# Seven products for eight in 13 pairs of weight blocks of the two output projections of a two-layer attention trunk

## The chip, the cores and the metric

The kernel runs on one core of one Trainium2 chip. The metric is the device time of one execution in microseconds (us). Three runs of the kernel before gave 1759.19, 1760.52 and 1760.68 us. Five engines take part: TensorE (PE) multiplies matrices, VectorE (DVE) and ScalarE (ACT) work on elements, GpSimd (POOL) issues most of the small transfers, and SyncE (SP) issues the large ones.

## The reference

The input x has 256 rows of 2048 columns. Layer A projects it to queries, keys, values and gates of 4096 columns each and runs chunked attention in 32 heads of 128. Layer B takes queries and gates, and shared keys and values, from the rows that layer A leaves, and runs a causal attention with forget gates. Each layer ends in an output projection from 4096 to 2048 columns, which is added to x:

```python
x = x + (o * silu(g)) @ a_w_out      # layer A: o is (256, 4096), a_w_out is (4096, 2048)
...
x = x + (o * silu(g)) @ b_w_out      # layer B, the same shapes
...
out = rms_norm(x, final_norm)        # over the 2048 columns
```

Everything is float32.

## The kernel before, in words

**The three products.** PE multiplies float32 numbers of a reduced format (fp32r) here, so each factor is split in two: `hi` is the number rounded to that format, `lo` is what is left. A product is made of three matmuls, x_hi·w_hi, x_hi·w_lo and x_lo·w_hi (`mm3`, L182). Each matmul multiplies 128 rows of K by a 128x512 piece of weights.

**The stream of weights.** All weights are read once from HBM, in blocks of 512 KB: 128 partitions x 1024 numbers, that is two chunks of K (`KB` = 2, called j = 0 and 1) of 512 output columns. SP issues one transfer for a block into a `raw` tile (L203). There are three such tiles (`RAW`), taken in turn, so the transfer of a block waits until the block three before it has been split. ACT writes `hi` (L237) and DVE writes `lo` = raw - hi (L238), into one of four pairs of tiles (`SPLIT`), and waits until PE is done with the block that was in it. Since the rows are two halves of 128 (t = 0 and 1), a block makes 2 (j) x 2 (t) x 3 = 12 matmuls. The class `Feed` keeps three blocks split ahead of PE.

**The output projections.** `ao` (layer A) and `bo` (layer B) have four units each, ao0 to ao3 and bo0 to bo3: a unit is 512 output columns, 16 blocks (0 to 15), and two accumulators in PSUM, acc0 and acc1, for the two row halves. `project` goes through the blocks in an order that is written out by hand, `ao_order` and `bo_order`: unit after unit, with one exception: the last block of bo0 comes eight blocks into bo1. In bo3 the last eight blocks (`LATE`) multiply only t = 0 at first; their t = 1 matmuls come at the very end, so the row half t = 0 can be finished while PE still works. Five of these blocks (8 to 12) stay in tiles of their own (`KEPT`, called keep8 to keep12).

**The residual tile.** Four blocks before the end of a unit, `load_xin` has SP load the 512 KB of x that the unit is added to into `xin` (L617). All units share one buffer of this tile: the load for the next unit waits until everything has read it.

- In ao, DVE adds the accumulators (L626) and SP stores the sum to HBM as x1 (`x1d`, L627). Layer B needs x1 turned by 90 degrees. For units 0 to 2 that goes by a transposition on DVE (`xinY`), transfers from POOL and splits (L148, L149) some blocks later. For unit 3, PE transposes (L167), right at the first block of the next stage, which is called bqg0.
- In bo, DVE adds (L762), ACT sums the squares (`junk`, L763), and DVE multiplies with the final gain into `xg` (L765). After unit 3, `finish_tile` (L776 to L788) makes the row factor out of four sums (`fin`), scales `xg` and stores it, first for t = 0 and then for t = 1.

**Order.** The program is written as one sequence; a scheduler of the framework assigns each engine its instructions in an order of its own making. Each engine takes its instructions strictly in that order, and an instruction that waits holds up all behind it. This holds for SP and its transfers too.

Of the kernel before, what the change touches and what calls it, by code (L numbers as in the profile page):

```python
# [49 lines left out]
BIG = 8  # L50
TERMS = 8
HEAT = 9
WAIT = 8
# [10 lines left out]
def r32(ap):  # L64
    return ap.bitcast(F32)
# [8 lines left out]
def trunk(ctx, tc, x, x_t, gains, a_w_in, a_rel, a_w_out, kv_w, f_w, f_b, b_w_in, b_w_out, final_norm, out):  # L74
# [98 lines left out]

    def mm3(acc, lhs, k, ts, hi, lo, nk, begun):

        parts = [(lhs.h(k), hi), (lhs.h(k), lo), (lhs.l(k), hi)]
        steps = [(t, i) for t in ts for i in range(3)]
        if k < KB:
            steps = [(t, i) for i in (0, 2, 1) for t in ts]
        for t, i in steps:  # L180
            x, w = parts[i]
            pe.matmul(acc[t], x[:, t * P:(t + 1) * P], w,  # L182
                      start=t not in begun, stop=k == nk - 1 and i == 2)
            begun.add(t)

    class Feed:
# [19 lines left out]
        def begin(self, first=None):  # L206
            spec, b = next(self.todo, (None, 0))
            if spec:
                load, *splits = self.also.get((spec["name"], b), (None, None, None))
                if load:  # L210
                    load()
                self.loaded.append((spec, b, self.load(spec, b, first), splits))

        def prepare(self, ahead=True, parts=(slice(None),)):
            if not self.loaded:
                self.begin()
            if not self.loaded:
                return
            spec, b, raw, (before, behind) = self.loaded.pop(0)
            if before:  # L220
                before()
# [41 lines left out]
        def get(self):  # L263
            self.fill()
            return self.ready.pop(0)

    def spec(name, w, nk, late=0, kept=0, g0=None):


        return dict(name=name, w=w, nk=nk, late=late, kept=kept, g0=g0)  # L270
# [13 lines left out]
    ao = [spec(f"ao{u}", a_w_out[u], KI) for u in range(4)]  # L284
    for sp_ in ao:
        todo += whole(sp_)
    for g in range(NG):
# [3 lines left out]
    for sp_ in qkvg[2 * NG:]:  # L291
        todo += whole(sp_)
    ao_order = [i for sp_ in ao for i in whole(sp_)]
    bo_order = [i for sp_ in bo for i in whole(sp_)]
    bo_order.insert(KI // KB + WAIT, bo_order.pop(KI // KB - 1))
    todo += bo_order
    feed = Feed(todo)
    order = iter(qkvg)

    class Unit:  # L300
# [8 lines left out]
        def step(self, b):  # L309
            hi, lo = feed.get()  # L310
            hold = b >= self.nk // KB - self.late
            if hold:
                self.held.append((b, hi, lo))
            for j in range(KB):
                mm3(self.acc, self.lhs, b * KB + j, range(1 if hold else NT), cols(hi, j), cols(lo, j), self.nk,
                    self.begun)
            self.left -= 1
            if not self.left:
                for b, hi, lo in self.held:
                    for j in range(KB):  # L320
                        mm3(self.acc, self.lhs, b * KB + j, [1], cols(hi, j), cols(lo, j), self.nk, self.begun)

# [8 lines left out]

    def project(lhs, order, begun, closed, sides):


        units = {}
        for sp_, b in order:
            u = int(sp_["name"][-1])
            if u not in units:
                units[u] = Unit(lhs, sp_)
            units[u].step(b)  # L340
            begun(u, b)
# [6 lines left out]
            if not units[u].left:  # L348
                more = closed(u, units[u].acc)
                if more:  # L350
                    sides.append(more)
        for side, _ in sides:
# [40 lines left out]

    def attention(g, biases, qk, vg, half, ocat, queues=(pool,) * NQ, line=(None, None), home=None):

# [60 lines left out]
        act.activation(hi, oT, AF.Copy)  # L456
        dve.tensor_sub(lo, oT, r32(hi))
        yield

# [79 lines left out]
    def side_a(g, accs):  # L539
# [16 lines left out]

        yield from attention(g, biases, qk, vg, halfA, oA, (pool, pool, pool, act), (2, 2), home)

# [59 lines left out]

    def ao_begun(u, b):
        if b == 11:  # L620
            load_xin(xf, u)

    def ao_closed(u, acc):
        cs, xin = slice(u * UN, (u + 1) * UN), xins.pop(u)
        for t in range(NT):
            dve.tensor_add(xin[:, t], acc[t], xin[:, t])  # L626
# [11 lines left out]

    project(oA, ao_order, ao_begun, ao_closed, [(prev, [2, 6, 2, 1])])
    tot1 = const.tile([P, NT], F32, name="tot1")  # L640
# [74 lines left out]
    def side_b(g, accs):  # L715
# [17 lines left out]
        evac_scaled(kv, 0, GC, rsB, qk[:, :, GC:])  # L733
        rest_of = attention(g, biases, qk, lambda: (v, gs), halfB, oB, line=(1, 2), home=home)
        next(rest_of)
# [66 lines left out]

    project(oB, bo_order, bo_begun, bo_closed, [(old, [1, 1, 0]), (prev, [4, 2, 1, 1, 1, 7, 2, 1])])

# [44 lines left out]
```

## Time and profile before

| what | value |
|---|---|
| runs before | 1759.19, 1760.52, 1760.68 us, median 1760.52 |
| profiled execution, its own time | 1762.27 us |
| its span | 1760.4 us |
| mean granted PE clock | 0.998 |
| PE busy in the span | 1746.0 us, 99% |
| DVE, ACT, POOL busy | 66%, 62%, 29% |
| HBM read | 351.05 MB, 202 GB/s over the span |

The busy time of an engine is the time in which an instruction of it was executing. Rows of a timeline give start, duration, engine, line, operation, what is written and read, and the shape. A row of a group gives line, engine, operation, shape and count, then total busy time and the mean of one in ns, then the idle time of the engine ahead of these instructions and what ended it. A name of a tile in a row leaves its numbers out, so `ao_raw` stands for all blocks of ao.

### The profile page before, as it was taken

What the parts mean: (1) busy time and instruction counts of PE and PEld (TensorE: products, weight loads), DVE (VectorE), ACT (ScalarE), POOL (GpSimd) and SP (SyncE); (2) the same over time, 40 slices, a digit from 0 to 9 for tenths busy, and PEclk for the clock granted to TensorE, in tenths of its full rate; (3) what the DMA queues carried; (4) which work ended last, traced back from release to release, by engine and by line L of the source; (5) the groups of instructions that cost most, each with busy time, mean ns of one, the idle gap of its engine ahead of it and who ended that gap; (6) DMA issues with size and microseconds to landing.
All of it is one profiled execution on the core that took longest, in us unless ns stands there. A gap on an engine that the chain in (4) does not pass through costs nothing.

```text
span 1760.4 us, 25526 instructions
## 1 busy us (share of the span) xinstructions
PE 1746.0 (99%) x8387; PEld 1533.1 (87%) x8387; DVE 1159.1 (66%) x1662; ACT 1084.1 (62%) x2063; POOL 515.7 (29%) x1071
## 2 busy tenths in 40 slices
PE   9999999999999999999999999999999999999997
PEld 7888888888888888888888888888888888888886
DVE  6666666666666666655666777777777777776654
ACT  6555555555555555555556777777777777765443
POOL 1333333333333333111104333333333333333000
PEclk9999999999999999999999999999999999999999
DMA  7867776777777777777766777777777777776665
GB/s 255 248 218 227 225 225 224 225 224 224 223 224 224 224 225 222 222 239 240 239 195 226 236 227 222 227 224 226 223 228 226 227 222 231 249 225 222 216 217 161
DMA packets 143652, 396.34 MB, mean 225 GB/s; under 512 B 31104, under 2 KB 38560, under 8 KB 143392
## 3 DMA queue, kind: packets, MB, share of 16 engines
q1 hardware_dynamic: 107472, 354.25, 63.8%
q0 software_dynamic: 32256, 37.29, 6.6%
q10 hardware_dynamic: 3792, 3.17, 0.6%
q8 instruction: 66, 1.08, 0.2%
q14 instruction: 66, 0.54, 0.1%
HBM read 351.05 MB, written 4.23 MB: 202 GB/s over the span
## 4 chain that ended last, share of the span: by engine, by line
PE 94%; DMA 2%; DVE 2%; ACT 1%; issue 0%; POOL 0%; SPq 0%; ACTq 0%; DVEq 0%; POOLq 0%
PE bkv_acc L182 19%; PE bqg_acc L182 19%; PE avg_acc L182 18%; PE aqk_acc L182 17%; PE ao_acc L182 9%; PE bo_acc L182 8%; DMA bo_raw<-in_b_w_out 1%; PE op L448 1%; PE s0p L414 1%; PE op L391 0%; PE s1p L390 0%; PE s1p L391 0%; PE op L392 0%; PE op L390 0%; PE s1p L392 0%
## 5 line engine op out<-in xcount | busy, mean ns | idle before, releaser
L363 POOL DMA_DIRECT2D sgZ<-sgY x512 | 250.9, 497 | 194.6 <-DVE sgY L360 96.5
L363 POOL DMA_DIRECT2D turned<-turned x448 | 219.9, 498 | 267.7 <-PE avg_acc L182 93.0
L233 DVE SCALAR_TENSOR_TENSOR bqg_lo<-bqg_raw,gain,bqg_hi 128x512 fp32r<-128x512 f32 x256 | 182.0, 747 | 97.1 <-ACT bqg_hi L232 97.0
L232 ACT ACTIVATE bqg_hi<-bqg_raw,gain 128x512 fp32r<-128x512 f32 x256 | 170.9, 714 | 114.1 <-PE bqg_acc L182 50.2
L238 DVE TENSOR_TENSOR avg_lo<-avg_raw,avg_hi 128x1024 fp32r<-128x1024 f32 x127 | 153.4, 1219 | 115.6 <-ACT avg_hi L237 115.5
L238 DVE TENSOR_TENSOR aqk_lo<-aqk_raw,aqk_hi 128x1024 fp32r<-128x1024 f32 x125 | 152.4, 1219 | 92.7 <-ACT aqk_hi L237 92.6
L233 DVE SCALAR_TENSOR_TENSOR bkv_lo<-bkv_raw,gain,bkv_hi 128x512 fp32r<-128x512 f32 x256 | 181.3, 748 | 45.3 <-ACT bkv_hi L232 42.3
L237 ACT ACTIVATE avg_hi<-avg_raw 128x1024 fp32r<-128x1024 f32 x127 | 132.5, 1055 | 124.5 <-PE aqk_acc L182 60.1
L182 PE MATMUL bqg_acc<-bqg_hi,x1Th 128*128 128x512 f32 x512 | 191.6, 384 | 0.0
L182 PE MATMUL aqk_acc<-aqk_hi,xTh 128*128 128x512 f32 x512 | 190.9, 383 | 0.2
L182 PE MATMUL aqk_acc<-aqk_lo,xTh 128*128 128x512 f32 x512 | 189.0, 379 | 1.2 <-DVE aqk_lo L238 1.2
L182 PE MATMUL avg_acc<-avg_hi,xTh 128*128 128x512 f32 x512 | 190.2, 382 | 0.0
L182 PE MATMUL avg_acc<-avg_lo,xTh 128*128 128x512 f32 x512 | 188.9, 379 | 0.3 <-DVE avg_lo L238 0.3
L182 PE MATMUL bqg_acc<-bqg_hi,x1Tl 128*128 128x512 f32 x512 | 189.1, 379 | 0.0
L182 PE MATMUL bkv_acc<-bkv_hi,x1Th 128*128 128x512 f32 x512 | 189.0, 379 | 0.0
L182 PE MATMUL aqk_acc<-aqk_hi,xTl 128*128 128x512 f32 x512 | 188.9, 379 | 0.0
L182 PE MATMUL avg_acc<-avg_hi,xTl 128*128 128x512 f32 x512 | 188.8, 379 | 0.0
L182 PE MATMUL bkv_acc<-bkv_lo,x1Th 128*128 128x512 f32 x512 | 188.8, 379 | 0.0
L182 PE MATMUL bkv_acc<-bkv_hi,x1Tl 128*128 128x512 f32 x512 | 188.8, 379 | 0.0
L182 PE MATMUL bqg_acc<-bqg_lo,x1Th 128*128 128x512 f32 x512 | 188.8, 379 | 0.0
L237 ACT ACTIVATE aqk_hi<-aqk_raw 128x1024 fp32r<-128x1024 f32 x125 | 131.5, 1052 | 91.9 <-PE avg_acc L182 44.0
L232 ACT ACTIVATE bkv_hi<-bkv_raw,gain 128x512 fp32r<-128x512 f32 x256 | 168.8, 711 | 27.9 <-PE bqg_acc L182 21.4
(205 smaller groups left out, 3442.4 us busy)
## 6 DMA issues: line engine op xcount, KB each, us to landing
bqg_raw<-in_b_w_in SPq DMA_DIRECT2D x128, 512.0 KB, 4.3
bkv_raw<-in_kv_w SPq DMA_DIRECT2D x128, 512.0 KB, 4.0
avg_raw<-in_a_w_in SPq DMA_DIRECT2D x127, 512.0 KB, 4.3
aqk_raw<-in_a_w_in SPq DMA_DIRECT2D x125, 512.0 KB, 3.4
ao_raw<-in_a_w_out SPq DMA_DIRECT2D x64, 512.0 KB, 4.2
bo_raw<-in_b_w_out SPq DMA_DIRECT2D x64, 512.0 KB, 4.2
sgZ<-sgY POOLq DMA_DIRECT2D x512, 40.0 KB, 4.0
turned<-turned POOLq DMA_DIRECT2D x448, 32.0 KB, 3.5
```

What stands on the lines that cost most here:

```text
L182: pe.matmul(acc[t], x[:, t * P:(t + 1) * P], w, start=t not in begun, stop=k == nk - 1 and i == 2)
L232: act.activation(hi[:, :, j], raw[:, :, j], AF.Copy, scale=gk)
L233: dve.scalar_tensor_tensor(lo[:, :, j], raw[:, :, j], gk, r32(hi[:, :, j]), op0=OP.mult, op1=OP.subtract)
L237: act.activation(hi[:, :, j], raw[:, :, j], AF.Copy)
L238: dve.tensor_sub(lo[:, :, j], raw[:, :, j], r32(hi[:, :, j]))
L363: queues[j].dma_start(out=r32(z)[j * SQ:(j + 1) * SQ, i], in_=y[i * SQ:(i + 1) * SQ, j])
L414: pe.matmul(s0p[:, i], q0[:, i], qkT[:, HG + i, 0], start=True, stop=True)
L448: pe.matmul(op[:, i, P:], v1[:, i * DH:(i + 1) * DH], pT[:, i, NT], start=False, stop=i == HG - 1)
```

## The change

Thirteen times, one block of a unit and the block with the same number of its neighbour are taken together as a *quad*. The two blocks hold four pieces of weights: B11 and B21 (unit a, j = 0 and 1), B12 and B22 (unit b). The rows hold four pieces of x: A11 and A12 (t = 0), A21 and A22 (t = 1). Plainly that is eight products, and 24 matmuls. The quad makes them out of seven products, so 21 matmuls, in the form of Strassen and Winograd: four sums of pieces of x, four differences of pieces of weights, and sums of products.

- **Loading and splitting.** `Quad.load` (L283) brings both blocks, two transfers of 512 KB, into one tile `quad0`, of which there is only one. `Quad.split` gives four items, 0 to 3: B11 with B21; the two differences in `quad1` (written at L289); B22; and two further differences, that are written over pieces of `quad0` (L290, L298). Item 2 is 128x512, the others are 128x1024. Each is split by ACT (L295, hi0 to hi3) and DVE (L296, lo0 to lo3) into the same four pairs of tiles as the blocks. Quads don't count towards the three raw tiles.
- **Products.** Three of the seven go straight to an accumulator of a unit. The other four, p1, p5, p6 and p7, are shared between accumulators, so they add up over all quads of a pair of units in four banks of PSUM that the attention uses, too. After the last quad of a pair, ACT copies p1, and four adds of DVE make the four corrections out of them (`comb`, L337 to L341), in the tile `quad1`. At the end of each unit DVE adds its half of them to `xin` (128x1024, L752 and L926) ahead of the accumulators (L754, L891).
- **Sums of x.** The four sums are made for the first five groups of heads in each attention (`sum_up`): five small operations on DVE and one on ACT more for each.
- **Order.** Quads take the place of blocks 0 to 2 of ao0 and ao1, of blocks 0 to 4 of ao2 and ao3, and of blocks 0 to 4 of bo2 and bo3; Q0 is the first quad of a pair. bo0 and bo1 have none. The order (a and b being the two units of a pair) is now, for ao0 and ao1: a3 to a14, b3, Q0, b4, b5, a15, Q1, b6 to b8, Q2, b9 to b15. For the other two pairs: a5 to a8, Q0, a9 to a11, Q1, a12 to a14, Q2, b5 to b7, Q3, a15, b8, b9, Q4, b10 to b15. Unit a now ends with the last quad.

Two places show what that does to the order on the engines. At the end of ao, SP stands as follows. Before, the residual tile of ao3 (here `xin_8058`) was loaded some nine transfers before the first block of bqg0, the first stage of layer B:

```order
L617 DMA xin_8058<-in_x 128x2x512
L203 DMA ao3_raw8_7862<-in_a_w_out 128x1024
...
L203 DMA ao3_raw15_7998<-in_a_w_out 128x1024
L203 DMA bqg0_raw0_8021<-in_b_w_in 128x1024
...
L203 DMA bqg0_raw5_8124<-in_b_w_in 128x1024
L627 DMA x1d_6770<-xin_8058 128x512 x2
```

Now the stores of ao2's sum (`xin_7841`) stand behind two blocks of bqg0, and the load for ao3 (`xin_8147`) another block later:

```order
L204 DMA ao3_raw15_8070<-in_a_w_out 128x1024
L204 DMA bqg0_raw0_8115<-in_b_w_in 128x1024
L204 DMA bqg0_raw1_8133<-in_b_w_in 128x1024
L755 DMA x1d_6808<-xin_7841 128x512 x2
L204 DMA bqg0_raw2_8153<-in_b_w_in 128x1024
L744 DMA xin_8147<-in_x 128x2x512
L204 DMA bqg0_raw3_8173<-in_b_w_in 128x1024
```

So this load moved from ahead of ao3's last eight blocks to behind them, and behind three blocks of bqg0. On PE, the transpositions of ao3's sum stood behind the first matmul of bqg0:

```order
L182 MATMUL ao_acc_7821<-ao_hi_8060,oAl_182 128x512
L182 MATMUL bqg_acc_8190<-bqg_hi_8078,x1Th_6772 128x512
L167 MATMUL xT_8142<-ident,xin 128x128
L167 MATMUL xT_8147<-ident,xin 128x128
L182 MATMUL bqg_acc_8191<-bqg_hi_8078,x1Th_6772 128x512
```

They now stand behind nine of them:

```order
L183 MATMUL ao_acc_7624<-ao_hi_8149,oAl_182 128x512
L183 MATMUL bqg_acc_8300<-bqg_hi_8167,x1Th_6810 128x512
...
L183 MATMUL bqg_acc_8300<-bqg_hi_8167,x1Tl_6812 128x512
L168 MATMUL xT_8232<-ident,xin 128x128
L168 MATMUL xT_8237<-ident,xin 128x128
L183 MATMUL bqg_acc_8301<-bqg_hi_8167,x1Tl_6812 128x512
```

The transpositions thus stand eight matmuls further on. The second place is the end of bo. Before, SP loaded the residual tile of bo3 (`xin_16633`) ten blocks from the end:

```order
L203 DMA bo3_raw5_16424<-in_b_w_out 128x1024
L617 DMA xin_16633<-x1d_6770 128x2x512
L203 DMA bo3_raw6_16454<-in_b_w_out 128x1024
...
L203 DMA bo3_raw15_16605<-in_b_w_out 128x1024
L788 DMA out_0<-xg0_15431 128x512 x2
```

Now it comes last, and Q4's two transfers (`bo_quad0`) stand behind the block for keep10:

```order
L204 DMA bo3_raw10_16681<-in_b_w_out 128x1024
L283 DMA bo_quad0_15582<-in_b_w_out 128x2x512 x2
L204 DMA bo3_raw11_16692<-in_b_w_out 128x1024
...
L204 DMA bo3_raw15_16779<-in_b_w_out 128x1024
L744 DMA xin_16823<-x1d_6808 128x2x512
L917 DMA out<-xg_15579 128x512 x2
```

On DVE, before, the splits of keep8 to block 15 ran one after the other, with nothing between them:

```order
L238 TENSOR_TENSOR bo3_keep11_16591<-bo3_raw11_16543,bo3_keep11_16591 128x1024
L238 TENSOR_TENSOR bo3_keep12_16602<-bo3_raw12_16560,bo3_keep12_16602 128x1024
L238 TENSOR_TENSOR bo3_lo13_16614<-bo3_raw13_16577,bo3_hi13_16613 128x1024
L238 TENSOR_TENSOR bo3_lo14_16624<-bo3_raw14_16594,bo3_hi14_16623 128x1024
L238 TENSOR_TENSOR bo3_lo15_16636<-bo3_raw15_16605,bo3_hi15_16635 128x1024
```

The same engine has this from Q4's first item on:

```order
L296 TENSOR_TENSOR quad_lo0_16711<-bo_quad0_15582,quad_hi0_16710 128x1024
L289 TENSOR_TENSOR bo_quad1_15583<-bo_quad0_15582 128x1024
...
L246 TENSOR_TENSOR bo3_keep11_16768<-bo3_raw11_16692,bo3_keep11_16768 128x1024
...
L296 TENSOR_TENSOR quad_lo3_16748<-bo_quad0_15582,quad_hi3_16747 128x1024
L246 TENSOR_TENSOR bo3_lo13_16804<-bo3_raw13_16760,bo3_hi13_16803 128x1024
L338 TENSOR_TENSOR bo_quad1_15583<-bo_quad1_15583,p6_16374 128x512
L246 TENSOR_TENSOR bo3_lo14_16814<-bo3_raw14_16771,bo3_hi14_16813 128x1024
L246 TENSOR_TENSOR bo3_keep12_16776<-bo3_raw12_16700,bo3_keep12_16776 128x1024
...
L926 TENSOR_TENSOR xin_16567<-xin_16567,bo_quad1_15583 128x1024
L246 TENSOR_TENSOR bo3_lo15_16826<-bo3_raw15_16779,bo3_hi15_16825 128x1024
```

The splits of the last blocks now share DVE with those of Q4, and with the corrections and the residual of bo2 (`xin_16567`). The diff, cut to its core (the code of `sum_up`, of `open` and of the names that only passed a parameter is left out):

```diff
     def mm3(acc, lhs, k, ts, hi, lo, last, begun):
...
         def begin(self, first=None):
             spec, b = next(self.todo, (None, 0))
-            if spec:
+            if isinstance(b, Quad):
+                b.load()
+                self.loaded += [(spec, (b, i), None, (None, None)) for i in range(4)]
+            elif spec:
...
         def refill(self):
-            while len(self.loaded) < RAW:
+            while sum(raw is not None for _, _, raw, _ in self.loaded) < RAW:
...
+    class Quad:
...
+        def load(self):
+            q = self.all
+            for r in range(2):
+                sp.dma_start(out=q.raw[:, :, r], in_=q.w[self.units[r]][self.b])
+
+        def split(self, i):
+
+            raw, t = self.all.raw, self.all.t
+            if not i:
+                dve.tensor_sub(t[:, 0], raw[:, :, 1], raw[:, :, :, 0])
+                dve.tensor_sub(raw[:, :, 1, 0], raw[:, :, 1, 1], t[:, 0, :, 0])
+            src = [raw[:, :, 0], t[:, 0], raw[:, :, 1, 1:], raw.rearrange("p a r j n -> p a (r j) n")[:, :, 1:3]][i]
...
+            act.activation(hi[:, :, :n], src, AF.Copy)
+            dve.tensor_sub(lo[:, :, :n], src, r32(hi[:, :, :n]))
+            if not i:
+                dve.tensor_sub(raw[:, :, 0, 1], raw[:, :, 0, 1], raw[:, :, 1, 0])
+            return hi, lo
...
+            if self.first:
+                q.p = [bank(n) for n in ("p1", "p5", "p7", "p6")]
...
+            w = feed.get()
+            prod(p1, x(0, 0), w, 0)
+            add(first, 0, x(1, 0), w, 1)
+            w = feed.get()
+            prod(p5, sx(0), w, 0)
+            prod(p7, sx(2), w, 1)
+            w = feed.get()
+            add(second, 0, sx(3), w, 0)
+            w = feed.get()
+            add(first, 1, x(1, 1), w, 0)
+            prod(p6, sx(1), w, 1)
+            if self.last:
...
+                act.activation(c[:, 0], p1, AF.Copy)
+                dve.tensor_add(c[:, 3], c[:, 0], p6)
+                dve.tensor_add(c[:, 2], c[:, 3], p5)
+                dve.tensor_add(c[:, 1], c[:, 3], p7)
+                dve.tensor_add(c[:, 3], c[:, 1], p5)
...
+            normal = a[:-1] + b[:3] + a[-1:] + b[3:]
...
+    ao_order = ao_quads.order(ao[0], ao[1], 3, 13) + ao_quads.order(ao[2], ao[3], QUADS, 4)
...
+    bo_order = whole(bo[0]) + whole(bo[1])
     bo_order.insert(KI // KB + WAIT, bo_order.pop(KI // KB - 1))
+    bo_order += bo_quads.order(bo[2], bo[3], QUADS, 4)
...
+        if g < QUADS:
+            quads.sum_up(oT)
...
-    def ao_begun(u, b):
-        if b == 11:
+    def ao_begun(u, left):
+        if left == 4:
             load_xin(xf, u)
...
+        dve.tensor_add(xin, xin, ao_quads.comb[:, u % 2 * NT:u % 2 * NT + NT])
...
-    def bo_begun(u, b):
-        if b == (11 if u else 14):
+    def bo_begun(u, left):
+        if left == (4 if u else 1):
             load_xin(x1d, u)
...
+        if u > 1:
+            dve.tensor_add(xin, xin, bo_quads.comb[:, u % 2 * NT:u % 2 * NT + NT])
```

More of the change, by code (lines that the diff above doesn't have):

```diff
@@ L51 @@
 TERMS = 8
+QUADS = 5
 HEAT = 9
@@ L182, in mm3 @@
             pe.matmul(acc[t], x[:, t * P:(t + 1) * P], w,
-                      start=t not in begun, stop=k == nk - 1 and i == 2)
+                      start=t not in begun, stop=last and i == 2)
             begun.add(t)
@@ L219, in prepare @@
             spec, b, raw, (before, behind) = self.loaded.pop(0)
+            if raw is None:
+                self.ready.append(b[0].split(b[1]))
+                self.refill()
+                return
             if before:
@@ new lines, in trunk, with __init__, order, open @@
+    class Quads:
+        def __init__(self, name, w):
+            self.name, self.w, self.sums = name, w, []
+        def order(self, first, second, n, lead):
+            a, b = ([(sp_, i) for i in range(n, sp_["nk"] // KB)] for sp_ in (first, second))
+            normal = a[:-1] + b[:3] + a[-1:] + b[3:]
+            units = [int(sp_["name"][-1]) for sp_ in (first, second)]
+            out = normal[:lead]
+            for i in range(n):
+                out.append((None, Quad(self, units, i, not i, i == n - 1)))
+                out += normal[lead + 3 * i:lead + 3 * i + 3] if i < n - 1 else normal[lead + 3 * i:]
+            return out
+        def open(self):
+            self.raw = big_tile([P, IL, 2, KB, HN], F32, f"{self.name}_quad0")
+            self.t = big_tile([P, 2, IL, KB, HN], F32, f"{self.name}_quad1")
+        def sum_up(self, oT):
+            if len(self.sums) % 2 == 0:
+                self.tile = big_tile([P, 2, 2, 4, P], F32R, f"{self.name}_sums{len(self.sums)}")
+            self.sums.append(self.tile[:, len(self.sums) % 2])
+            hi, lo = self.sums[-1][:, 0], self.sums[-1][:, 1]
+            v = att.tile([P, 4, P], F32, name="v_sums", tag="wideh")
+            a11, a21, a12, a22 = (oT[:, k, t * P:(t + 1) * P] for k in range(KB) for t in range(NT))
+            dve.tensor_add(v[:, 0], a21, a22)
+            dve.tensor_sub(v[:, 2], a11, a21)
+            dve.tensor_sub(v[:, 1], v[:, 0], a11)
+            dve.tensor_sub(v[:, 3], a12, v[:, 1])
+            act.activation(hi, v, AF.Copy)
+            dve.tensor_sub(lo, v, r32(hi))
@@ L313, in step @@
                 self.held.append((b, hi, lo))
+            self.left -= 1
             for j in range(KB):
-                mm3(self.acc, self.lhs, b * KB + j, range(1 if hold else NT), cols(hi, j), cols(lo, j), self.nk,
-                    self.begun)
-            self.left -= 1
+                mm3(self.acc, self.lhs, b * KB + j, range(1 if hold else NT), cols(hi, j), cols(lo, j),
+                    not self.left and j == KB - 1, self.begun)
             if not self.left:
@@ L330, in rest, with project, get @@
             yield u.acc
-    def project(lhs, order, begun, closed, sides):
+    def project(lhs, specs, order, begun, closed, sides):
         units = {}
+        def get(u):
+            if u not in units:
+                units[u] = Unit(lhs, specs[u])
+            return units[u]
         for sp_, b in order:
[L337 to L341, printed above, removed]
+            if sp_:
+                us = [int(sp_["name"][-1])]
+                get(us[0]).step(b)
+            else:
+                us = b.units
+                b.step(lhs, *(get(u) for u in us))
+            for u in us:
+                begun(u, units[u].left)
             for side, steps in sides:
@@ L347, in project @@
                         steps.pop(0)
[L348 to L351, printed above, removed]
+            for u in us:
+                if not units[u].left:
+                    more = closed(u, units[u].acc)
+                    if more:
+                        sides.append(more)
         for side, _ in sides:
```

43 lines of the change are left out of this document (32 added, 11 removed).

## The prediction

> **What bounds the kernel now.** I read the page first: its first part, and the shares of the chain that ended last.
>
> ```profile
> PE 1746.0 (99%) x8387; PEld 1533.1 (87%) x8387; DVE 1159.1 (66%) x1662; ACT 1084.1 (62%) x2063; POOL 515.7 (29%) x1071
> PE 94%; DMA 2%; DVE 2%; ACT 1%; issue 0%; POOL 0%; SPq 0%; ACTq 0%; DVEq 0%; POOLq 0%
> ```
>
> PE is busy for 99% of the span, and 94% of the last chain is PE. So I asked what PE waits for; the columns are total us, times, and the longest:
>
> ```profile
> PE op L390 <- ACT wideh L382: 1.9, 1, 1.9
> PE heat L108 <- DVE zeros L105: 1.3, 1, 1.3
> PE aqk_acc L182 <- DVE aqk_lo L238: 1.2, 2, 0.9
> PE bo_acc L182 <- DVE bo_lo L238: 0.8, 1, 0.8
> PE avg_acc L182 <- DVE avg_lo L238: 0.3, 1, 0.3
> ```
>
> That is 5.5 us in 1760. All splits and transfers are hidden behind matmuls. The time is the number of matmuls by their pace, plus the end. The pace is read from the timeline of ao, from the first to the last of 117 matmuls in a row:
>
> ```profile
> 839.76 0.38 PE L182 MATMUL ao_acc<-ao_hi,oAh 128*128 128x512 f32 x1
> ...
> 864.80 0.38 PE L182 MATMUL ao_acc<-ao_hi,oAl 128*128 128x512 f32 x1
> ```
>
> 25.04 us by 116 steps is 0.216 us (the 0.38 overlap). A block of 12 takes 2.59 us, a quad of 21 takes 4.53.
>
> **The change part by part.** *Matmuls removed.* 13 quads by 3 matmuls are 39, by 0.216: -8.4 us. This is all that the change can gain; each wait that it opens on PE is taken from that.
>
> *Work added to DVE and ACT.* The groups by shape give the means (ns, after the comma), and the DMA view of 770 to 860 us the transfers (us to landing, last); the row below those is a window at the start (us, then busy times; GB/s last).
>
> ```profile
> L238 DVE TENSOR_TENSOR ao_lo<-ao_raw,ao_hi 128x1024 fp32r<-128x1024 f32 x64 | 78.1, 1222 | 67.5 <-ACT ao_hi L237 67.2
> L457 DVE TENSOR_TENSOR oAl<-oT,oAh 128x512 fp32r<-128x512 f32 x16 | 11.1, 692 | 11.1 <-ACT oAh L456 11.1
> L626 DVE TENSOR_TENSOR xin<-ao_acc,xin 128x512 f32<-128x512 f32 x8 | 5.1, 682 | 0.0
> L765 DVE SCALAR_TENSOR_TENSOR xg<-xin,gfin 128x512 f32<-128x512 f32 x8 | 5.2, 684 | 0.1
> L149 DVE TENSOR_TENSOR x1Tl<-xinZ,x1Th 128x128 fp32r<-128x128 f32 x24 | 5.8, 284 | 0.0
> L237 ACT ACTIVATE ao_hi<-ao_raw 128x1024 fp32r<-128x1024 f32 x64 | 67.5, 1055 | 74.3 <-PE ao_acc L182 48.3 <-DMA ao_raw<-in_a_w_out 23.8 <-PE avg_acc L182 2.2
> L456 ACT ACTIVATE oAh<-oT 128x512 fp32r<-128x512 f32 x16 | 10.1, 630 | 31.3 <-DVE oT L452 31.3
> ...
> ao_raw<-in_a_w_out SPq DMA_DIRECT2D x35, 512.0 KB, 4.2
> x1d<-xin SPq DMA_DIRECT2D x4, 256.0 KB, 4.8
> xin<-in_x SPq DMA_DIRECT2D x2, 512.0 KB, 6.2
> ...
> 14.00:16.00 2.00, 2.00 (x11) 1.76 (x10) 1.77 (x4) 2.00 (x6) 0.00 (x0) 1.00 1.03 413
> ```
>
> No row shows the new subtractions; by shape they are nearest to the splits: 1.22 us for 128x1024, 0.69 for half of it. The sums of x in ten groups of heads cost DVE 4 x 0.28 + 0.69 and ACT 0.63 in each; DVE is busy for 66% and ACT for 62%, so I take 0 (0 to 0.5, for a group where a split comes late by it).
>
> A quad costs DVE four splits (3 x 1.22 + 0.69) and three differences (1.22 + 2 x 0.69), 6.95 us in all. With the three blocks between two quads that is 10.6 us, against 4.53 + 3 x 2.59 = 12.3 on PE. As throughput it fits. But there is one tile `quad0`: the next quad can be loaded only when lo3 has read it, and the loop through this tile is a first transfer, hi0 (1.06), and DVE's 6.95. (The second transfer lands 1.3 us after the first at the earliest, 512 KB at 413 GB/s, and hides behind hi0 and lo0.) With a transfer of 4.2 us, as for `ao_raw`, the loop is 12.2 us. That is 0.1 under PE's 12.3. Nine quads run in such a loop (two, four, and three of bo's; its Q4 is told below). Only where layer B's turned x comes in, 8 x 0.28 us of DVE work near the second pair's first quads, do I expect a wait: +0.7. The bounds are 0, and with 4.8 for a transfer (the x1d row) 9 x 0.5 = 4.5.
>
> *The end of ao.* T is when PE ends the last quad there. DVE must have split lo3 by then, and has three block splits queued behind; I take them as done at T+2. Then come three corrections (3 x 0.68), a block split (1.22), the fourth correction (0.68), the add to `xin` (1.22, as the split of that shape): T+7.2. Another block split and two accumulators: T+8.4, 9.1, 9.8. The stores of x1 land 4.8 us later, T+14.6. Only then can SP, where this load now stands behind ao3's last blocks, load `xin` for ao3, and three blocks of bqg0 wait behind it. At 4.2 us it lands at T+18.8; the two adds (1.22 + 0.68) bring it to T+20.7. PE reaches the transpositions after six blocks and nine matmuls, at T + 15.5 + 1.9 = 17.4. It waits for 3.3 us. Before, it lost some 0.3 here (a matmul of 0.22, then nothing until 879.10):
>
> ```profile
> 878.61 0.38 PE L182 MATMUL bqg_acc<-bqg_hi,x1Th 128*128 128x512 f32 x1
> ...
> 879.10 0.41 PE L167 MATMUL xT<-ident,xin 128*128 128x128 f32 x2
> ```
>
> So +3.0. The bounds: 1.2, if the stores land within the 3.0 us of the row for `out` below, and 5.0, if the load takes 6.2.
>
> *The end of bo.* These are the rows of its transfers, and of the end:
>
> ```profile
> out<-xg SPq DMA_DIRECT2D x4, 256.0 KB, 3.0
> xin<-x1d SPq DMA_DIRECT2D x1, 512.0 KB, 4.6
> ...
> 1740.13 0.48 PE L182 MATMUL bo_acc<-bo_lo,oBh 128*128 128x512 f32 x1 [0.78 <-DVE bo_lo L238]
> 1741.51 0.69 DVE L762 TENSOR_TENSOR xin<-bo_acc,xin 128x512 f32<-128x512 f32 x1 [1.44 <-PE bo_acc L182]
> 1745.05 0.16 DVE L781 SCALAR_TENSOR_TENSOR fin<-fin 128x1 f32<-128x1 f32 x1
> 1751.46 0.38 PE L182 MATMUL bo_acc<-bo_hi,oBl 128*128 128x512 f32 x1
> 1752.60 0.63 ACT L763 ACTIVATE junk<-xin 128x512 f32<-128x512 f32 x1 [6.02 <-DVE xin L762]
> 1753.13 0.19 ACT L763 ACTIVATION_READ_ACCUMULATOR junk<-xin 128x1 f32 x1
> 1754.13 0.16 DVE L781 SCALAR_TENSOR_TENSOR fin<-fin 128x1 f32<-128x1 f32 x1
> 1754.33 1.33 ACT L785 ACTIVATE xg<-xg,fin 128x512 f32<-128x512 f32 x2 [0.68 <-DVE fin L781]
> ```
>
> I count from U, when PE starts Q3. Without any new wait PE would take 2 x 4.53 for the quads, 2.59 for a15 and 8 x 2.59 for blocks 8 to 15, 32.4, then the wait of 0.8 that is there now, and 8.7 from the last matmul to the end of the span (1751.46 + 0.22 to 1760.4): U+41.9.
>
> Now the working of the new order. Between Q3 and Q4 stand a15 and only the t = 0 halves of blocks 8 and 9, so PE reaches Q4 at U + 4.5 + 2.6 + 2.6 = 9.7. By the loop above Q3's lo2 is done at U+1.0 (hi3 and lo3 of Q2 2.3 us after Q2's start, then 4.2 for the transfer, 1.06 for hi0 and 5.7 for DVE's six operations up to lo2, less 12.3); I take U+1.4, for the hand-overs. DVE then splits keep8 (U+2.6) and Q3's lo3 (U+3.9). Only now is the tile free. Q4's first transfer lands at U+8.1, hi0 at 9.2, lo0 at 10.4, the first differences at 12.3; DVE's order puts keep11's split there (13.5), then a difference (14.2), lo1, lo2 and lo3 (17.3). PE, with the last four matmuls behind lo3, ends Q4 at U+18.2, and with some hand-overs between ACT and DVE that I round up, at 18.5. Without the wait that would be U+15.1 (9.7 + 4.5, and four matmuls of keep8 that stand in between): 3.4 us.
>
> After it DVE has block 13 (18.6), a correction behind PE's last product (19.5), block 14, keep12 (21.9), three corrections (24.0), the add to bo2's `xin` (25.2), block 15 (26.5), two accumulators and two multiplications for `xg` (29.2, at 0.68 each). Then the tile is free, and the load for bo3 can start. It lands 4.2 us later (U+33.5; the `xin` row says 4.6, but nothing stands before it now). Add and accumulator: 35.4; from there to `fin` of t = 0 is 3.0 (1742.20 to 1745.21): 38.4. The accumulator of t = 1 follows in DVE's order (39.1), but ACT first scales `xg` (1.33: 39.7), then squares (0.8: 40.5); `fin` takes 1.0 (1753.32 to 1754.29), and from there to the end are 6.1 (1754.33 to 1760.4): U+47.6. That is +5.7 over 41.9; PE's wait of 3.4 is inside this. The bounds: 3.3, if Q4's transfer and the last load take 3.0 each, and 8, with 4.8 and a hand-over of 0.1 at each of ten steps.
>
> *Sum.* -8.4 + 0.7 + 3.0 + 5.7 = +1.0 us. The profiled execution has 1762.27 us of its own, and would have 1763.3. The median of the runs shown is 1.75 lower, 1760.52, and I add the same to that: **1761.5 us**. With the terms' bounds, seldom all on one side, this case runs from 1757 to 1767.
>
> **The rivals.** *Lone transfers land early* (faster). Both new waits are behind transfers that stand alone in SP's queue. The 4.2 us is measured with others under way, and 3.0 stands for stores of half the size, which speaks for some gain. Then the sum is -8.4 + 0 + 1.2 + 3.3 = -3.9, 1756.6; if PE waited nowhere, 1752.1. Against it: DVE's chain after Q4, 10 us of work in a written order, contains no transfer.
>
> *The tile of the quads becomes the bound* (slower). The place is `quad0`, the loop of 12.2 against 12.3 us. It decides from a first transfer of 4.3 us. Blocks now arrive five in 12.3 us, where there were 4.75, and the view gives 6.2 us for a load between others. At 5.2 us PE waits 0.9 in each of nine quads, 8.1 in place of 0.7: 1769. Against it: SP has waited for this tile, so few transfers are under way when it is loaded.
>
> *The clock falls in the new waits.* These are windows of the end; the column behind the engines is the granted clock.
>
> ```profile
> 1752.00:1753.00 1.00, 0.00 (x0) 0.00 (x0) 0.97 (x2) 0.40 (x1) 0.00 (x0) 1.00 0.00 0
> 1753.00:1754.00 1.00, 0.00 (x0) 0.00 (x0) 0.79 (x4) 0.62 (x3) 0.00 (x0) 1.00 0.00 0
> 1754.00:1755.00 1.00, 0.00 (x0) 0.00 (x0) 0.93 (x4) 0.67 (x2) 0.00 (x0) 0.59 0.00 0
> ```
>
> The clock falls about 2.3 us after the last matmul's end (1751.84). The longest wait in between, 1.9 us, left no trace. A wait of 3.3 us at the end of ao is longer than 2.3. If the clock then stays low for as long as PE stood, half of 3 us is lost, 1.5; twice, if Q4's pieces count as well: 1763 to 1764.5. Against it: at Q4 a few matmuls stand between the pieces of the wait. The Trainium skill (TensorE: Matmul & The Clock Gate, "HAM oscillation — how this bites in real kernels") says that PE must not idle for over some 3.4 us, or the clock is halved for the next window. By that rule a wait of 3.3 us is just short of costing anything, and one past it would cost 1.7 us, an estimate from that page. The trace agrees that idleness drops the clock; how long it stays low afterwards no row here shows.
>
> **How the numbers follow.** A measurement of this kernel can tell about 0.2%, 3.5 us, from no change: 1757 to 1764. Chances: the forecast 0.55, early transfers 0.2, the tile 0.15, the clock 0.1. Faster by over 0.2%: 0.04 of the forecast and 0.16 of early transfers, 0.20. Slower: 0.13 of the forecast (bounds of the two ends), 0.13 of the tile, 0.07 of the clock, 0.33. The rest, 0.47, is within it. The range is 1755 to 1768: it takes in the forecast's bounds, most of the early transfers and all of the clock, and leaves out the case of no waits and the worst of the tile, together under 0.2.
>
> **What would show it.** In the profile after, PE's matmuls should be 39 fewer; PE should wait for about 3 us at the transpositions behind bqg0's ninth matmul, released by DVE's add to `xin`, with SP's load waiting for x1d; for 3 us in pieces within bo's Q4; and the last matmul (U+18.5, 80 matmuls still to go, and a wait of about 1 for block 15, which makes U+36.8) should stand some 11 us ahead of the end of the span in place of 8.7. Waits of 0.5 us and more on lo0 or lo1 in each quad would mean the tile. A granted clock under 1.00 at 890 us would mean the clock. The forecast is wrong if the transpositions come without a wait, or if bo3's `xin` is loaded before the corrections of bo2 are done.

## The result and the profile after

| | before | after |
|---|---|---|
| median of 6 runs | 1760.60 us (1759.19 to 1763.19) | 1767.93 us (1766.77 to 1769.72) |
| profiled execution, its own time | 1762.27 | 1766.88 |
| its span | 1760.4 | 1765.2 |

The changed kernel takes 1.0042 times as long as the kernel before, with a 95% interval of 1.0029 to 1.0055. It is slower, by some 7 us in the medians and by 4.6 in the two profiled executions. The page of the changed kernel, its first part and the shares of its last chain:

```profile
PE 1740.3 (99%) x8348; PEld 1526.1 (86%) x8348; DVE 1239.6 (70%) x1795; ACT 1107.6 (63%) x2102; POOL 515.2 (29%) x1071
PE 91%; DMA 4%; DVE 2%; ACT 1%; issue 1%; POOL 1%; SPq 0%; ACTq 0%; DVEq 0%; POOLq 0%
```

The 39 matmuls are gone (8387 to 8348). The chain that ended last is PE for 91% instead of 94%: the share of transfers in it rose from 2% to 4%. What PE waits for, the longest of the list behind the start of the kernel:

```profile
PE xT L168 <- DVE xin L754: 3.6, 1, 3.6
PE ao_acc L515 <- ACT quad_hi L295: 1.6, 1, 1.6
PE p L515 <- ACT quad_hi L295: 1.4, 1, 1.4
PE ao_acc L516 <- DVE quad_lo L296: 1.2, 2, 0.8
PE bo_acc L183 <- DVE bo_keep L246: 0.8, 1, 0.8
```

With those of the start, the list adds up to 14.0 us, where it was 5.5. Three places make up the difference, and a fourth loss is not in the list.

**The end of ao.** PE's timeline around the transpositions of ao3's sum, and two windows (the granted clock is the number behind the engines):

```profile
882.10 0.41 PE L168 MATMUL xT<-ident,xin 128*128 128x128 f32 x2 [3.57 <-DVE xin L754]
...
884.44 0.63 PE L183 MATMUL bqg_acc<-bqg_lo,x1Th 128*128 128x512 f32 x1
884.87 0.63 PE L183 MATMUL bqg_acc<-bqg_hi,x1Tl 128*128 128x512 f32 x1
...
887.06 0.38 PE L183 MATMUL bqg_acc<-bqg_hi,x1Tl 128*128 128x512 f32 x1
887.27 0.38 PE L183 MATMUL bqg_acc<-bqg_hi,x1Th 128*128 128x512 f32 x1
```

```profile
884.00:885.00 1.00, 1.00 (x4) 0.80 (x3) 0.57 (x1) 1.00 (x4) 0.00 (x0) 0.50 0.96 361
888.00:889.00 1.00, 1.00 (x6) 0.87 (x5) 1.00 (x6) 1.00 (x6) 0.00 (x0) 1.00 1.09 180
```

PE waits 3.57 us, and then the clock is at 0.50: two matmuls start 0.43 us apart (884.44, 884.87), and 0.21 apart again three microseconds later. In windows of 1 us from 883 to 886 the clock was 0.63, 0.50, 0.50 and 0.66, so 1.71 us of full clock were lost. No list of waits shows that.

**The second quad of ao's second pair.** ScalarE, VectorE and PE there:

```profile
820.02 0.51 ACT L149 ACTIVATE x1Th<-xinZ 128x128 fp32r<-128x128 f32 x2 [2.88 <-DMA xinZ<-xinY]
820.44 1.04 ACT L295 ACTIVATE quad_hi<-ao_quad 128x1024 fp32r<-128x1024 f32 x1
821.51 1.22 DVE L296 TENSOR_TENSOR quad_lo<-ao_quad,quad_hi 128x1024 fp32r<-128x1024 f32 x1 [0.65 <-ACT quad_hi L295]
821.53 0.48 PE L515 MATMUL ao_acc<-quad_hi,oAh 128*128 128x512 f32 x1 [1.57 <-ACT quad_hi L295]
822.79 0.48 PE L516 MATMUL ao_acc<-quad_lo,oAh 128*128 128x512 f32 x1 [0.78 <-DVE quad_lo L296]
```

ScalarE stands idle for 2.88 us in front of the turned x1 of ao1 (`x1Th<-xinZ`), whose transfer has not landed. The split hi3 of Q1 stands behind it in ScalarE's order and starts as soon as it is done (820.44). PE waits 1.57 for hi3 and 0.78 for lo3.

**The end of bo.** PE, SyncE, VectorE and ScalarE from Q4 on:

```profile
1730.99 0.70 PE L515 MATMUL p<-quad_hi,bo_sums 128*128 128x512 f32 x2 [1.44 <-ACT quad_hi L295]
1735.56 0.38 PE L517 MATMUL p<-quad_hi,bo_sums 128*128 128x512 f32 x1
1746.34 0.53 SPq L744 DMA_DIRECT2D xin<-x1d  x1
1750.32 1.23 DVE L926 TENSOR_TENSOR xin<-xin,bo_quad 128x1024 f32<-128x1024 f32 x1 [3.79 <-DMA xin<-x1d]
1753.87 0.38 PE L183 MATMUL bo_acc<-bo_hi,oBl 128*128 128x512 f32 x1
1755.26 0.16 DVE L910 SCALAR_TENSOR_TENSOR fin<-fin 128x1 f32<-128x1 f32 x1
1758.95 1.33 ACT L914 ACTIVATE xg<-xg,fin 128x512 f32<-128x512 f32 x2 [0.68 <-DVE fin L910]
```

Q3 starts at 1718.25, which is U of the prediction. Q4's last matmul starts at U+17.3, bo3's residual is loaded at U+28.1, and the span ends at U+46.95. The last matmul stands 11.3 us ahead of the end. The load is issued right behind VectorE's last read of bo2's residual; VectorE then waits 3.79 us for it.

### The profile page after: what moved, and what is told of

It reads as the page before. It is cut to its first block, busy times and chain, and to the rows that moved or that the text cites. A ratio compares the mean times of both kernels' runs of the same rounds, so it can differ in the third digit from the quotient of the medians.

```text
span 1765.2 us, 25639 instructions
## 1 busy us (share of the span) xinstructions
PE 1740.3 (99%) x8348; PEld 1526.1 (86%) x8348; DVE 1239.6 (70%) x1795; ACT 1107.6 (63%) x2102; POOL 515.2 (29%) x1071
## 4 chain that ended last, share of the span: by engine, by line
PE 91%; DMA 4%; DVE 2%; ACT 1%; issue 1%; POOL 1%; SPq 0%; ACTq 0%; DVEq 0%; POOLq 0%
PE bkv_acc L183 19%; PE bqg_acc L183 19%; PE aqk_acc L183 18%; PE avg_acc L183 18%; PE bo_acc L183 6%; PE ao_acc L183 4%; DMA xinZ<-xinY 1%; DMA bo_raw<-in_b_w_out 1%; PE s0p L539 1%; PE op L573 1%; DMA ao_raw<-in_a_w_out 0%; PE op L516 0%; PE s1p L516 0%; PE s1p L515 0%; PE s1p L517 0%
```

## The experiments

Two theories were on record before the first runs: that the loss is a sum of separate waits, at the places above, and that each quad costs by itself, wherever it stands. Times are compared by the ratio to the kernel before, run on the same chip. The ratio and its 95% interval come from the single runs and can differ from the ratio of the two medians, by 0.0007 at most here. How much a kernel is faster than the changed one is the difference of two ratios; where their intervals overlap (the changed kernel's is 1.0029 to 1.0055), the times alone don't show it.

**Two blocks fewer ahead of bo's quads** (`bo_lead2`):

```diff
-    bo_order += bo_quads.order(bo[2], bo[3], QUADS, 4)
+    bo_order += bo_quads.order(bo[2], bo[3], QUADS, 2)
```

> One number changed: in the last two units of bo two blocks instead of four stand ahead of the first quad, so Q0 to Q4 come two blocks earlier, three whole blocks (7.8 us of PE) stand between Q3 and Q4, and blocks 8 to 15 all come behind Q4. Theory A (the loss is made of waits at three places, priced by the profile: 3.1 us in the first two quads of ao's second pair, 3.3 of waiting and 1.6 of lower clock at the end of ao, 5.0 at the end of bo, against 8.4 gained): the 5.0 at the end of bo go nearly all, the rest stays; about 1763 us, 4 to 5 less than the changed kernel's 1767.9. In its trace Q4 has no wait, and the last matmul stands some 9 us ahead of the end in place of 11.3. Rival B (quads cost by themselves, evenly: the 15.7 us between the 8.4 gained and the 7.3 lost, by 13, are 1.2 us for each quad wherever it stands): no change by more than 0.5 us, 1767.5 to 1768.5.

Measured: 1.0027 (1.0016 to 1.0037), some 2.6 us less than the changed kernel; the intervals overlap. From the last projection matmul ahead of bo to the end the profile has 178.8 us in place of 180.8: Q4's wait shrank to 0.66, and the last matmul stands 9.1 us ahead of the end. But VectorE is now late with the splits of blocks 13 to 15 (three waits of 0.15 to 0.25), since the corrections are still among them, and a wait of 0.86 early in bo (1592.8 us) is new. So the profile shows that the place was the right one; the price of 4 to 5 us was too high, and part of what is removed at Q4 comes back.

**No quads in bo** (`ao_only`): bo's four units in plain order, without corrections and sums.

> The eight quads of ao stay; bo has none, and the sums of x in layer B's attention go with them. Theory A: five quads of bo gain 5 x 3 x 0.216 = 3.2 and cost 5.0 at the end, so without them the time falls by 1.8, to about 1766; the end of ao keeps its wait of about 3.5 us and the half clock behind it. Rival B (1.2 us for each quad against a gain of 0.65): five quads fewer give 2.8 us back, to about 1765. Rival C (what costs is mostly bo, or the sums of x in layer B's attention): 1760 or less.

Measured: 1.0031 (1.0019 to 1.0043), 1766.1 us. That is the first theory's number, by which bo's five quads are worth about 2 us less than nothing, and in the trace the end of ao keeps its wait (3.85 us) and the half clock behind it. But the 1765 of a price for each quad lies within this interval too, and the interval overlaps that of the changed kernel, so this run only excludes the third case, 1760 or less.

**The turn of ao's second unit four blocks later** (`late_turn`):

```diff
-        return more and (more, [8, 1, 1, 1])
+        return more and (more, [12 if u == 1 else 8, 1, 1, 1])
```

> One number changed: the four steps that split the turned x1 of ao's second unit begin twelve blocks behind its end in place of eight, so on ScalarE they stand behind the splits of Q1 in the second pair, and not ahead of hi3. Theory A: the waits of 1.6 and 0.8 us in that quad go, and nothing else: about 1765.5, 2.4 less than the changed kernel. Rival B (the tile of the quads is the bound there, and ScalarE's wait for the turned x1 lies beside it): the quad waits all the same, within 0.5 of 1767.9.

Measured: 1.0026 (1.0015 to 1.0036), some 2.8 us less than the changed kernel, near the 2.4 expected, though the intervals overlap. The trace is clearer: both waits of Q1 are gone. The waits for ao's quads that are left in its trace are these two:

```profile
PE ao_acc L516 <- DVE quad_lo L296: 0.4, 1, 0.4
PE p L516 <- DVE quad_lo L296: 0.4, 1, 0.4
```

So the order on ScalarE held the quad up, and not the quads' tile. "And nothing else" did not hold: the wait at the transpositions grew from 3.57 to 4.69 us, so that part of the gain is lost again there.

**Tiles of their own for the last residuals** (`xin2`):

```diff
-        xins[u] = att.tile([P, NT, UN], F32, name="xin", tag="R")
+        if u == 3:
+            xins[u] = [att.tile([P, UN], F32, name=f"xin3{t}", tag=tag) for t, tag in enumerate(("oT", "gs"))]
...
```

The rest of the edit hands on two halves in place of one tile: for the last unit the load and the add of the corrections go in two pieces.

> The residual of the last unit of each projection gets two tiles of its own (128x512 each, in places that the attention has left by then), so its load waits for nothing; all else as in the changed kernel. Theory A: at the end of ao the wait of 3.6 us falls to some 0.5, and the 1.6 us of half clock behind it go; at the end of bo the load of 4 us leaves the chain, and the last matmul (11.3 us ahead of the end now) decides again with 8.9, 2.4 less. Together 7 us less: about 1761. Rival B (SyncE's load is hidden behind something else that is late, the corrections on VectorE): 1 to 2 us less at most, 1766 to 1767. Rival D (only the clock matters, the wait would come back elsewhere in stage B): 2 us less.

Measured: 1.0011 (1.0003 to 1.0020), some 5.5 us less than the changed kernel, and the intervals don't overlap. PE's wait at the transpositions fell to 1.68, no low clock followed in this execution, and the last matmul stands 9.4 us ahead of the end:

```profile
881.19 1.28 DVE L770 TENSOR_TENSOR xin<-ao_acc,xin 128x512 f32<-128x512 f32 x2
882.02 0.41 PE L168 MATMUL xT<-ident,xin 128*128 128x128 f32 x2 [1.68 <-DVE xin L770]
```

The residual's one buffer is the largest single cause. The 1.68 that stay come from VectorE's order: the last add stands behind a split of bqg0 whose block landed late.

**Both of these** (`late_xin2`).

> All thirteen quads, with the later turn of ao's second unit and the tiles of their own for the residual of the last units, together. Theory A (the waits are separate and add up): 8.4 gained, against 0.8 in the first quad of ao's second pair, 1.4 that is left at the end of ao (the adds stand behind a split of bqg0 that waits for its block), and 2.8 that is left in bo: 3.4 less than the kernel before, about 1757.7. From the two single experiments, 2.8 and 5.5 less than the changed kernel, it would be 1760. Rival B (what is freed in one place is waited for in the next): as the better of the two alone, about 1763.

Measured: 1.0001 (0.9992 to 1.0010), 1761.6 us. The two single effects together (2.8 and 5.5 less) would make 0.9995, which is within this interval; against the better of the two alone, 1.0011, the gain is not clear of both intervals. The sum from waits was too good by 4 us. The transpositions waited 2.18 us this time, with a low clock after.

**Ten quads, with blocks behind the last one** (`fewer`): four quads in ao's second pair and three in bo's, and the later turn.

```diff
-    ... + ao_quads.order(ao[2], ao[3], QUADS, 4)
-    bo_order += bo_quads.order(bo[2], bo[3], QUADS, 4)
+    ... + ao_quads.order(ao[2], ao[3], 4, 4)
+    bo_order += bo_quads.order(bo[2], bo[3], 3, 4)
```

> Ten quads instead of thirteen: three in ao's first pair as before, four in its second pair and three in bo's pair, so that in both pairs the first unit ends with a whole block behind its last quad and nine or more blocks still to come; and the later turn of ao's second unit. Theory A: ten quads gain 6.5 us; the transpositions at the end of ao and the last blocks of bo no longer wait, and some 0.8 us stay in the first quad of ao's second pair: 5.7 us less than the kernel before, about 1755.5. Rival B (each quad costs 1.2 us and gains 0.65): ten quads, 5.6 us more than the kernel before, about 1766.5.

Measured: 1.0005 (0.9996 to 1.0014), 1761.6 us: neither theory. bo did what the first one said: 177.5 us from the last projection matmul ahead of bo, 1.7 less than before, for three quads that are worth 1.9. At the end of ao a wait of the old size is back:

```profile
874.93 0.51 ACT L149 ACTIVATE x1Th<-xinZ 128x128 fp32r<-128x128 f32 x2 [1.23 <-DMA xinZ<-xinY]
877.42 0.48 DVE L150 TENSOR_TENSOR x1Tl<-xinZ,x1Th 128x128 fp32r<-128x128 f32 x2
877.82 1.28 DVE L754 TENSOR_TENSOR xin<-ao_acc,xin 128x512 f32<-128x512 f32 x2
878.65 0.41 PE L168 MATMUL xT<-ident,xin 128*128 128x128 f32 x2 [3.42 <-DVE xin L754]
```

The residual is there in time now (it landed at 869). But splits of ao2's turned x1 have moved ahead of the add on VectorE; the first waited for its transfer on ScalarE until 874.93, and splits of bqg0 lie between it and the add.

**Only the first pair's three quads** (`pair1_only`), the rest plain.

> Only the three quads of ao's first pair; ao's second pair and bo are plain, and the sums of x are made for the first three groups of heads of layer A alone. Theory A: these three quads opened no wait in the trace, so they give their whole gain, 9 matmuls by 0.216: 1.9 us less than the kernel before, about 1759.2. Rival B (0.56 us lost for each quad): 1.7 more, about 1762.8.

Measured: 1.0012 (1.0003 to 1.0021). These three had no wait in the changed kernel, and still do not pay here. The waits are in plain blocks behind them, where splits stand behind the turned x1 (0.84 and 0.62, and 0.3 for a split on ScalarE):

```profile
802.27 0.51 ACT L149 ACTIVATE x1Th<-xinZ 128x128 fp32r<-128x128 f32 x2 [2.31 <-DMA xinZ<-xinY]
805.10 0.48 PE L183 MATMUL ao_acc<-ao_lo,oAh 128*128 128x512 f32 x1 [0.84 <-DVE ao_lo L246]
```

These waits take what the quads gain, and no more: the profiled execution is one of the faster ones (1761.26 us, the median is 1762.96), and what the others lose on top is not known. From this I formed a further theory: that it costs to let the two units of a pair end close together.

**The sums alone** (`sums_only`): no quads; the sums are made and not used.

> No quads at all; the sums of x for the first five groups of heads are made in both attentions, and not used. Theory A: they lie beside matmuls; the same as the kernel before within 0.5 us, about 1761. Rival C (VectorE in the attentions comes late by them): 2 us more or above.

Measured: 0.9996 (0.9988 to 1.0005). The sums are hidden.

**The order alone** (`paired_plain`): each quad replaced by its two plain blocks; the sums and the corrections go with the quads.

```diff
-                out.append((None, Quad(self, units, i, not i, i == n - 1)))
+                out += [(first, i), (second, i)]
...
```

> No quads and no sums: only the order of the changed kernel. Where a quad stood there are now its two plain blocks, one of each unit, so all units end in the same places. Theory A2: the order alone costs some 2.5 in the first blocks of ao's second pair, 1 to 2 at the end of ao (the corrections are not there, so the stores go out 4 us earlier) and 1 to 2 at the end of bo: about 5 more than the kernel before, 1766 (1763.5 to 1768). Rival B (the quads' own work on VectorE and their one tile): as the kernel before within 1, 1760 to 1762.

Measured: 1.0003 (0.9994 to 1.0011). The theory of the pairs falls: without quads the same ends of units cost nothing that the times show, where 5 us were forecast. Only one of its three waits is in the trace, 1.59 us at the transpositions. What moves the turned x1 and the residual further must come with the quads. In this kernel ao2's sum is stored at 860.15 us and the load for ao3 issued at 866.45; in the changed kernel it is 869.54 and 874.60, behind the four corrections and the add of them on VectorE. That these alone do it is not shown, since the quads' loads and differences are gone here, too.

**The units far apart again** (`spread8`, `spread11`): all blocks of the first unit first, so that the second ends twelve blocks later; four quads in ao's second pair and four in bo's (`spread8`), and the same with ao's first pair and the later turn (`spread11`).

```diff
-            normal = a[:-1] + b[:3] + a[-1:] + b[3:]
+            normal = a + b if lead < 13 else a[:-1] + b[:3] + a[-1:] + b[3:]
...
```

> Eight quads, four in ao's second pair and four in bo's, none in ao's first; and in both pairs all blocks of the first unit come ahead of the second's, so the first unit ends with its fourth quad and the second twelve blocks (31 us) later, nearly as far apart as in the kernel before (41 us). Theory A2 (what costs is that the two units of a pair end close together: the turned x1 of the first is still in the way of the second's on GpSimd, ScalarE and VectorE, and the residual tile is late; the quads themselves cost nothing): eight quads gain 5.2, a small wait of about 0.7 stays where the turned x1 of ao's second unit meets the quads: 4.5 less than the kernel before, about 1756.5. Rival B (each quad costs 1.2 us and gains 0.65): 4.5 more, about 1765.5.

> The same, with the three quads of ao's first pair as in the changed kernel and the later turn of its second unit. Theory A2: eleven quads gain 7.1; the first pair's ends stay 18 us apart, which leaves about 0.8 in the first quad of the second pair, and 0.7 as in the kernel with eight: 5.6 less than the kernel before, about 1755.5. Rival B: 6.2 more, about 1767.

Measured: 1.0027 (1.0018 to 1.0037) and 1.0035 (1.0021 to 1.0049). The theory of the pairs missed by some 9 and 12 us. Both are near the numbers of the theory of a price for each quad, but their traces show new waits. bo3's residual now stands in SyncE's queue among the late blocks, which PE takes in 1.3 us each; it waits for ScalarE's last read of bo2's, and keep12's block behind it comes late. In `spread8`:

```profile
1731.51 0.53 SPq L744 DMA_DIRECT2D xin<-x1d  x1
1737.88 1.06 ACT L245 ACTIVATE bo_keep<-bo_raw 128x1024 fp32r<-128x1024 f32 x1 [4.85 <-DMA bo_raw<-in_b_w_out]
1738.99 0.72 PE L183 MATMUL bo_acc<-bo_keep,oBh 128*128 128x512 f32 x2 [3.08 <-ACT bo_keep L245]
```

**The first pair with the later turn** (`pair1_late`).

> The three quads of ao's first pair alone, as before, with the later turn of ao's second unit. Theory A2: of the 2.5 us that this kernel waited in the plain blocks of ao's second pair, for splits that stood behind those of the turned x1, the part of the second unit goes (0.8); 1.1 less than without the later turn, and together about 1 less than the kernel before, 1760 (1759 to 1761). Rival B: no change against that kernel, about 1763.

Measured: 1.0003 (0.9994 to 1.0012), some 1.6 us less than without the later turn, where 1.1 were expected; the intervals overlap. In the trace the wait of 0.62 is gone, and that of 0.84 is still there (0.83). The 1 us less than the kernel before that were forecast did not come in the times.

**All of them in one account.** If quads cost nothing but waits, a span follows from the kernel before: 1760.4, less 0.647 (3 x 0.216) for each quad, plus what the list of PE's waits has over 5.5, plus the clock lost ahead of the last matmul (1 - granted clock, summed over windows of 1 us), plus what the end, from the start of the last matmul on, has over 8.9. It is an account of the profiled executions, one for each kernel; the ratios are of all runs.

| kernel | quads | ratio | PE's waits | clock lost | end | span | by the account |
|---|---|---|---|---|---|---|---|
| before | 0 | 1 | 5.5 | 0 | 8.9 | 1760.4 | 1760.4 |
| after | 13 | 1.0042 | 14.0 | 1.7 | 11.3 | 1765.2 | 1764.6 |
| bo_lead2 | 13 | 1.0027 | 13.7 | 3.4 | 9.1 | 1765.1 | 1763.7 |
| ao_only | 8 | 1.0031 | 10.1 | 3.4 | 9.0 | 1764.2 | 1763.3 |
| late_turn | 13 | 1.0026 | 12.5 | 1.7 | 11.3 | 1763.3 | 1763.0 |
| xin2 | 13 | 1.0011 | 12.3 | 1.7 | 9.4 | 1763.1 | 1761.0 |
| late_xin2 | 13 | 1.0001 | 9.6 | 1.7 | 9.5 | 1760.1 | 1758.3 |
| fewer | 10 | 1.0005 | 9.6 | 1.7 | 9.1 | 1759.8 | 1759.9 |
| pair1_only | 3 | 1.0012 | 7.3 | 0 | 9.0 | 1759.5 | 1760.3 |
| pair1_late | 3 | 1.0003 | 4.3 | 0 | 9.0 | 1758.7 | 1757.4 |
| sums_only | 0 | 0.9996 | 5.6 | 1.7 | 9.0 | 1761.5 | 1762.2 |
| paired_plain | 0 | 1.0003 | 5.6 | 0 | 9.0 | 1760.5 | 1760.6 |
| spread8 | 8 | 1.0027 | 12.0 | 3.4 | 9.0 | 1764.9 | 1765.2 |
| spread11 | 11 | 1.0035 | 14.0 | 3.4 | 9.0 | 1766.9 | 1765.3 |

(The fall of `xin2` is not the one at the end of ao: it lies at 83 to 87 us, near the start.) It meets all spans within 2.1 us, most within 1.4, with no price for a quad. The five kernels with 13 quads lie 1.2 above it on average, so about 0.1 us of a quad's 0.65 is lost in steps that the account misses. That is little against the spread of the runs of one kernel (1759.19 to 1763.19 us before). Nor would a fixed price fit: the kernels with all 13 quads have ratios from 1.0001 to 1.0042. The gain is real in this account, and where the waits are goes by which instructions each order puts behind a late transfer. None of these kernels is faster than the kernel before by more than its interval.

## Why the prediction was right in part, and where it failed

**The matmuls.** -8.4 us was right: 39 are gone, and the account holds within 2.1 us with 0.65 for each quad.

**Work in the steady run.** +0.7 us was the term that failed; it measured 3.1 (0.31 + 0.41 in Q0 and 1.57 + 0.78 in Q1 of ao's second pair). The loop through `quad0` was judged rightly: the other quads in the loop had no wait to speak of. The step that failed is "only where layer B's turned x comes in, 8 x 0.28 us of DVE work". I counted this work, and not what its first instruction waits for: on ScalarE the splits of ao1's turned x1 stand ahead of hi3, and their transfers come late. `late_turn` removed the two waits of Q1.

**The end of ao.** The wait was forecast as 3.3 us and measured 3.57. The terms inside partly cancelled: the stores took 4.4 us (4.8 forecast), the load landed 5.25 us after it was issued (4.2), and VectorE was done with the accumulators at T+9.2 (9.8). `xin2` confirms the one buffer of the residual as the cause of about half of the wait: without it 1.68 us are left.

**The clock.** It was a rival with a chance of 0.1, and it came true: 1.7 us at the end of ao, near its price of 1.5. The sum had no term for it. The same order in ao has a second fall in the profiles of `bo_lead2` and `ao_only`, behind Q1's wait, and not in the changed kernel's own, the second fastest of its six runs. Another 1.7 us in some runs would explain part of why the medians differ by 7.3 us and the profiled executions by 4.6; the mean granted clock fits this (three of the six runs with 0.996 have 1768.8 us on average, the three with 0.997 have 1767.4), but it was not read out fall by fall in the other runs, so this stays open.

**The end of bo.** +5.7 us was forecast, and U+46.95 against 41.9 is +5.05. Q4 ended at U+17.5 (18.5 forecast), so it lost 2.4 us where 3.4 were forecast, the residual's load took 4.0 (4.2) and started at U+28.1 (29.3), and the last matmul stands 11.3 us ahead of the end (11).

**The sum.** Forecast were +1.0 for the profiled execution, measured +4.6: 2.4 from the quads behind the turned x1, 1.7 from the clock, less 0.7 at the end of bo, and some 0.2 here and there. So the likeliest case was not the one that came: the direction was that of its slower side (0.33). The measured 1767.93 lies above the 1757 to 1767 of that case, and inside the whole range, up to 1768, by 0.07 us; three of the six runs lie above it. That the range held was luck: the turned x1 and the clock cost 4.1 us more than the sum had for them, and the medians lie another 2.7 us further apart than the two profiles explain.

## What to carry to other kernels

Where one engine is busy for 99%, work that takes matmuls away paid here only as far as no instruction in another engine's written order ends up behind a late transfer; so read, for each engine that feeds the busy one, what stands ahead of the feeding instruction and what that waits for, and not only how long it takes. A buffer with one copy that is stored, freed and loaded again at the joint between two stages was the largest single cost here (5.5 us of the 7.3 came back with a place of its own for the last unit). And price each wait with the clock: each of 2.2 us or more cost 1.7 us on top.

## What the runs showed of the hardware that was not expected

The clock fell after much shorter waits than I had assumed. In the traces of all kernels here, each of the ten waits of PE of 2.2 to 4.7 us inside the run was followed by a stretch of half clock. Of eleven waits of 1.3 to 1.8 us three were (1.37, 1.55 and 1.67, each with another of 0.78 right after). Others of the same length were not, nor was the 1.95 us of the kernel before at 83 us: 1.57, with 0.78 right after, at 821 us in the changed kernel left the clock at 1.00, and 1.55 in `bo_lead2`, at the same instruction, was followed by 0.50. The same window of both, with the granted clock behind the engines:

```profile
825.00:826.00 1.00, 1.00 (x7) 0.86 (x6) 1.00 (x2) 0.10 (x1) 0.00 (x0) 1.00 1.03 371
```

```profile
825.00:826.00 1.00, 1.00 (x4) 0.81 (x3) 1.00 (x2) 0.63 (x3) 0.00 (x0) 0.50 0.88 313
```

The first of these rows is of the changed kernel, the second of `bo_lead2`: PE starts four matmuls in this microsecond in place of seven. Once it fell behind two shorter ones close together (0.83 and 0.63 at 81 to 82 us in `xin2`); 0.86 and 0.63 at the same place in `spread11` left it at 1.00. Each fall cost the same, 1.7 us, about 3.4 us at half clock. When it began differs: in the changed kernel 1.2 us after PE had started again, so the matmuls right behind the wait are not the slow ones; elsewhere up to 1.9 us after (`sums_only`), and in `spread11` ahead of PE's start at 881.48:

```profile
880.75:881.00 0.25, 0.00 (x0) 0.00 (x0) 0.25 (x1) 0.00 (x0) 0.00 (x0) 1.00 0.72 131
881.00:881.25 0.25, 0.00 (x0) 0.00 (x0) 0.25 (x2) 0.00 (x0) 0.00 (x0) 0.51 0.71 229
881.48 0.66 PE L168 MATMUL xT<-ident,xin 128*128 128x128 f32 x2 [3.32 <-DVE xin L754]
```

The Trainium skill (TensorE: Matmul & The Clock Gate, "HAM oscillation — how this bites in real kernels") gives some 3.4 us as the idle time that must not be exceeded. The 1.7 us that the prediction estimated for a fall agrees with the 1.70 to 1.71 of the traces; the threshold does not, and the measurement decides: here waits of 2.18 and 2.27 us were each followed by a fall, and so were all longer ones. What decides at 1.5 us was not tried.
